# Hybrid encoder block: the residual's rows loaded in the gates' stage, a second spread of the norm, and float32 parts of the mixers ahead of float32r ones

## The chip, the cores and the metric

The kernel runs on one core of one Trainium2 chip. A core has a tensor engine (PE; its weight loads are shown apart as PEld), a vector engine (DVE), a scalar engine (ACT), GpSimd (POOL) and a sync engine (SP) that here issues loads. The metric is the device time of one execution in microseconds, lower is better. A profile shows one execution; its span runs from the first to the last record.

## The reference

256 tokens of 2048 channels go through one layer: norm, one input projection, two token mixers (windowed attention with 8 query and 2 key heads; dilated attention with 12 heads in 3 groups of strides 1, 4 and 16), a gate on each, output projection, gated MLP with a convolution of width 3 on the gate, and a gated per-layer embedding.

```python
h = rms_norm(x, attn_norm[i])
proj = h @ w_in[i]
qa, ka, va, qb, kb, vb, ga, gb = jnp.split(proj, split_points, axis=-1)
ya = windowed_gqa(qa, ka, va, rel_bias_table, sink_a[i])
yb = dilated_attention(qb, kb, vb, rel_bias_table)
merged = jax.nn.sigmoid(ga) * (ya @ w_branch_a[i]) + jax.nn.sigmoid(gb) * (yb @ w_branch_b[i])
x = x + merged @ w_out[i]
hf = rms_norm(x, ffn_norm[i])
g = dwconv_centred(hf @ w_ffn_gate[i], conv_w[i], conv_b[i])
x = x + (jax.nn.gelu(g) * (hf @ w_ffn_up[i])) @ w_ffn_down[i]
gate_p = jax.nn.sigmoid(rms_norm(x, ple_norm[i]) @ w_ple_gate[i])
x = x + gate_p * (p[i] @ w_ple_proj[i])
```

All of it is float32. The logits of all heads get a bias from a table by relative position; the windowed heads have a sink in their softmax.

## The kernel before

**Weights.** All weights come as blocks of 128 x 128 in one long stream, in the order in which they are used. `load` brings 16 blocks (1 MB, `raw`, three buffers) on the sync engine's queue; in the opening in halves of 8. `split_to` (L181) makes of each sub of 8 blocks a float32r part `whi` on ACT (L190) and the rest `wlo` on DVE (L191), four buffers each. A projection of one block of channels (`product`, L207) takes per block a matmul with `whi` over 512 moving columns (high and low part of the activations) and one with `wlo` over 256 (L201, L202), 16 blocks each. Where the weights are the moving side (`wide_product`, L214), each step has two token halves with three matmuls (L224, L225, L226).

**Stages.** In the opening, seven projections run side by side over the input's channels as these land, and are summed in seven PSUM banks `first`; a small product for the bias table (L396) follows. `gather` (L249) then empties each `first` bank: ACT copies one half to `t` (L252), DVE adds the other (L256, L258). The value product of the windowed heads comes next and takes over the banks of the first two. Then come the mixers: one projection after the other, with attention put between their blocks. Next are the gates' stage (four rounds of both gates and both branch projections), the output projection, the MLP in two halves, and the embedding.

**What sets the order.** `at((job, step), f)` puts a piece of work in front of that step of that projection, and `run_due` runs it there. For each head or group, `attend` (L506) puts `scores` (L431) at step 9 of a projection, `turn` (L472; softmax weights transposed, L481, and split into `near` and `far`) at step 11 or 12 of the next, and `values` (L489) at step 4 of the one after. Near parts (`thrice`, L424) are three float32r matmuls each, L427 to L429; far parts, which only the groups with three heads have, are plain float32 (L446, L496). A scheduler then orders each engine's instructions; it may move an instruction far ahead of where it is written, unless it is marked with `keep`. Each DMA signals on one of eight signals in turn, so that an issue waits for the one eight places earlier on both queues together.

**Rows of the residual.** `fetch` (L667) loads a piece of 128 x 512 of the input's rows on ACT's queue into the buffer `x`, whose channel-wise content is then spent. It is written at step 6 of each gate's projection: eight pieces of 256 KB.

**The norm.** `rms` (L307) has two parts: `ask` computes the root, `tell` spreads it over all partitions with one float32 matmul (L304) and a copy on ACT (L315). The MLP's norm is spread once, at step 9 of its second projection.

Of the kernel before, what the change touches and what calls it, by code (L numbers as in the profile page):

```python
# [16 lines left out]
P = 128  # L17
T = 256
# [93 lines left out]
START = FIRST + 1  # L112
_JOBS = _plan()
WARM = 9


def _stream():
# [16 lines left out]
def _encoder(ctx: ExitStack, tc, xt, pt, cols, table, onehot, mask, ident_in, last_gain, wts, xrows, out):  # L134
# [172 lines left out]
    def rms(i, total, key, n):  # L307

        def ask():
            rc[key], dg = norm(total(), n)  # L310

            def tell():
                b = spread(dg)
                rt[key] = sc.tile([P, T], F32, name="rms")
                nc.scalar.activation(rt[key], b, AF.Copy)  # L315
            at(i[1], tell)
        at(i[0], ask)


# [2 lines left out]
    def at(i, f, *a):  # L322

        due.setdefault(i, []).append((f, a))
# [12 lines left out]
    hb = big.tile([P, QH * AW + BH * BW], F32, name="mov")  # L337
    hba = hb[:, :QH * AW].rearrange("p (h c) -> p h c", c=AW)
    hbb = hb[:, QH * AW:].rearrange("p (h c) -> p h c", c=BW)
    oh = ap_.tile([NBUCK, 2 * T], F32, name="oh", tag="near", bufs=1)  # L340
    tb = sc.tile([NBUCK, NH], F32, name="tb", bufs=1)
    mk = ap_.tile([NH, 2 * T], F32, name="mk", tag="s1", bufs=2)

# [67 lines left out]
    def view(a, offset, *dims):  # L411
        return bass.AP(tensor=a.tensor, offset=a.offset + offset, ap=[a.ap[0], *([step, n] for step, n in dims)])
# [18 lines left out]
    def scores(heads, y):  # L431

        n = len(heads)
        wide = T if n == 1 else 2 * T
        s = ap_.tile([P, 2, wide], F32, name="s", tag="s%d" % n, bufs=2 if n == 1 else 1)
        h, k = heads[0]
        sp = ps.tile([P, 2, T], F32, name="sp", bufs=2)
        for t in range(2):
            thrice(sp[:, t, :], [qs[h][:, c + t * P:c + (t + 1) * P] for c in (0, T)], [ks[k][:, :T], ks[k][:, T:]])
        a, step = (hba[:, h, :], P) if n == 1 else (hbb[:, h - QH, :], 1)  # L440
        nc.vector.tensor_tensor(s[:, :, :T], sp, view(a, 0, (step, 2), (1, T)), op=ALU.add)
        if n > 1:
            sp = ps.tile([P, 2, T], F32, name="sp", bufs=2)
            for g, (h, k) in enumerate(heads[1:]):
                for t in range(2):
                    nc.tensor.matmul(sp[:, t, g * P:(g + 1) * P], qs[h][:, t * P:(t + 1) * P],  # L446
                                     ks[k][:, (1 - t) * P:(2 - t) * P], start=True, stop=True)
            for g, (h, k) in enumerate(heads[1:]):
                nc.vector.tensor_tensor(s[:, :, T + g * P:T + (g + 1) * P], sp[:, :, g * P:(g + 1) * P],
                                        view(hbb[:, h - QH, :], 1, (0, 2), (2, P)), op=ALU.add)  # L450
        mx = ap_.tile([P, 2], F32, name="mx")
        nc.vector.tensor_reduce(mx, s, axis=AX.X, op=ALU.max)
        nm = ap_.tile([P, 2], F32, name="nm")
        if n == 1:
            sk = sinks[:, y:y + 1]
            nc.vector.tensor_scalar(nm, mx, sk, -1.0, op0=ALU.max, op1=ALU.mult)
        else:
            nc.vector.tensor_scalar(nm, mx, -1.0, None, op0=ALU.mult)
        den = ap_.tile([P, 2], F32, name="den")
        for t in range(2):  # L460
            nc.scalar.activation(s[:, t, :], s[:, t, :], AF.Exp, bias=nm[:, t:t + 1], accum_out=den[:, t:t + 1])
        if n == 1:
            es = ap_.tile([P, 2], F32, name="es")
            nc.scalar.activation(es, nm, AF.Exp, bias=sk)
            nc.vector.tensor_tensor(den, den, es, op=ALU.add)
        rd = ap_.tile([P, 2], F32, name="rd")
        nc.vector.reciprocal(rd, den)
        for t in range(2):
            nc.vector.tensor_scalar(s[:, t, :], s[:, t, :], rd[:, t:t + 1], None, op0=ALU.mult)
        return s  # L470

    def turn(s):  # L472

        n = s.shape[-1] // P
        near = ap_.tile([P, 2, 2, T], FR, name="near", bufs=1)
        far = ap_.tile([P, 2, T], F32, name="far", bufs=1) if n > 2 else None
        for c in range(0, n, 2):
            p = ps.tile([P, 2, T], F32, name="pt", bufs=2)
            for k in range(2):
                for t in range(2):  # L480
                    nc.tensor.transpose(p[:, k, t * P:(t + 1) * P], s[:, t, (c + k) * P:(c + k + 1) * P], ident)  # L481
            if c:
                nc.scalar.activation(far, p, AF.Copy)
            else:
                nc.scalar.activation(near[:, 0], p, AF.Copy)
                nc.vector.tensor_tensor(near[:, 1], p, near[:, 0].bitcast(F32), op=ALU.subtract)
        return near, far

    def values(w, heads, y):  # L489
        near, far = w  # L490
        o = ps.tile([P, T], F32, name="misc")
        for t in range(2):
            thrice(o, vs[heads[0][1]][t], [near[:, c, t, :] for c in range(2)], t == 0, t == 1 and len(heads) == 1)
        for g, (_, k) in enumerate(heads[1:]):
            for t in range(2):
                nc.tensor.matmul(o[:, t * P:(t + 1) * P], vs[k][1 - t], far[:, g, t * P:(t + 1) * P],  # L496
                                 start=False, stop=(g == len(heads) - 2), skip_group_check=True)
        hi, lo = yab[:, y, :T], yab[:, y, T:]
        if len(heads) == 1:
            ov = o[:, ::-1]  # L500
        else:
            ov, hi, lo = paired(o, True), pairs(hi), pairs(lo)
        nc.scalar.activation(hi, ov, AF.Copy)
        nc.vector.tensor_tensor(lo, ov, hi.bitcast(F32), op=ALU.subtract)

    def attend(i, heads, y):  # L506
        def first():
            s = scores(heads, y)

            def second():  # L510
                w = turn(s)
                at((i + 1, 11) if end else (i + 3, 4), values, w, heads, y)
            at((i + 1, 8) if end else (i + 2, 11 if len(heads) == 1 else 12), second)
        end = y == QH + HG - 1
        at((i + 1, 3 if end else 9), first)
# [4 lines left out]
    def after(job, i, acc, u=None):  # L520
        ff = held.get("ff")
        kind, n = job[0], job[1]
        if kind in ("q", "k", "v"):
# [35 lines left out]
                        else:  # L559
                            nc.vector.tensor_tensor(o, pairs(u), paired(r.bitcast(F32), True), op=ALU.subtract)  # L560
            else:
                r = ap_.tile([P, T], F32, name=kind, bufs=4 if kind == "q" else 7)
                nc.vector.tensor_tensor(paired(r, kind == "q"), pairs(u), pairs(rt[0]), op=ALU.mult)
            if kind == "k":
                ks[n] = r
# [99 lines left out]
    res = x.rearrange("p k t -> p (k t)").rearrange("p (t n) -> p t n", t=2)  # L665

    def fetch(t, c):  # L667
        nc.scalar.dma_start(res[:, t, c * W4:(c + 1) * W4], xrows[t][:, c * W4:(c + 1) * W4])

    movers = {  # L670
        "q": lambda k: hs[:, k, :], "g": lambda k: held["hf"][:, k, :],
# [7 lines left out]
    for i, job in enumerate(_JOBS):  # L679
# [25 lines left out]
            held["lg"] = spare[:, 2 * D:3 * D]  # L705
            nc.scalar.dma_start(held["lg"], last_gain)
        if kind == "g" and n == 0:
            rms([(i, 14), (i + 1, 9)], lambda: rowsums(held["ss1"]), 1, 2)
        if kind in ("ga", "gb"):
            at((i, 6), fetch, int(kind == "gb"), n)  # L710
        if kind == "bb":
# [10 lines left out]
            nc.vector.tensor_scalar(held["half"], root(rowsums(held["ss2"]), 2), 0.5, None, op0=ALU.mult)  # L722
        if i < FIRST:
            firsts[i] = gather(firsts[i], SCALE if kind == "q" else 1.0,
                               ap_.tile([P, T], F32, name="first", tag="k", bufs=7), keep)
            continue
        if i == FIRST:
            rms([(START, 6), (START, 12)], lambda: sums(tot, HALVES + TWINS), 0, 4)
# [91 lines left out]
```

## Time and profile before

| | |
|---|---|
| runs shown | 1495.14, 1496.67, 1497.42 us; median 1496.67 |
| profiled execution | 1494.23 us, span 1492.4 us |
| busy share of PE, PEld, DVE, ACT | 99%, 85%, 65%, 49% |
| HBM read | 279.49 MB, 189 GB/s over the span |
| granted PE clock | 0.997 on average |

The page has the busy time of each engine, the span in 40 slices, the DMA queues, the chain of work that ended last, the costliest groups of instructions, and the DMA issues. A row of the timeline has start, duration, engine, line, operation, output and inputs, and in brackets the idle time before it and what ended it. "ACTq" and "SPq" are the queues in which ACT and SP issue DMAs. A float32 product has two records per matmul. The records of matmuls overlap: in a dense stream the next starts before the last one's modelled end.

### The profile page before, as it was taken

To read this page: it belongs to the slowest core of one execution; us is meant where nothing else is said; L and a number is where in the kernel's file an instruction comes from. 1 tells how busy PE (TensorE), PEld (TensorE's weight loads), DVE (VectorE), ACT (ScalarE), POOL (GpSimd) and SP (SyncE) were. 2 spreads that over 40 slices of the span, in tenths; PEclk is the share of its full clock that TensorE was granted. 3 is DMA by queue.
4 is the path that set the end of the run, shared out by engine and by line. 5 is a ranking of instruction groups with operands and counts; after the bars stand their busy time and mean duration, and the time that the engine had idled before them with its cause. 6 is when DMAs were issued, how large, how long until landed. Compare 5 with 4: busy or idle time off the path is not lost.

```text
span 1492.4 us, 19451 instructions
## 1 busy us (share of the span) xinstructions
PE 1478.4 (99%) x7616; PEld 1261.6 (85%) x7616; DVE 976.3 (65%) x1406; ACT 728.3 (49%) x1031; POOL 3.7 (0%) x9
## 2 busy tenths in 40 slices
PE   9999999999999999999999999999999999999997
PEld 8888888888888888888888888888888888888886
DVE  6596665664554555578888885447787887555565
ACT  7465444444444444555554554334545554444553
POOL 0000000000000000000000000000000000000000
PEclk9999999999999999999999999999999999999999
DMA  8844444445554455454455455555544544544552
GB/s 305 297 170 150 165 173 178 168 166 190 193 198 180 186 197 198 178 222 180 190 198 190 179 196 197 196 192 178 196 181 186 193 179 194 188 181 196 190 188 102
DMA packets 46376, 282.89 MB, mean 190 GB/s; under 512 B 5124, under 2 KB 9988, under 8 KB 14028
## 3 DMA queue, kind: packets, MB, share of 16 engines
q1 hardware_dynamic: 44268, 277.31, 49.7%
q10 hardware_dynamic: 2016, 4.33, 0.8%
q8 instruction: 60, 0.98, 0.3%
q14 instruction: 32, 0.26, 0.0%
HBM read 279.49 MB, written 2.14 MB: 189 GB/s over the span
## 4 chain that ended last, share of the span: by engine, by line
PE 95%; DMA 2%; DVE 1%; ACT 1%; issue 0%; SPq 0%; POOL 0%; ACTq 0%; POOLq 0%; DVEq 0%
PE acc L201 28%; PE acc L224 17%; PE acc L225 17%; PE acc L226 16%; PE acc L202 14%; DMA raw<-in_wts 2%; PE pt L481 0%; PE pt L601 0%; DMA x<-in_xrows 0%; DVE wlo L191 0%; ACT whi L190 0%; PE misc L496 0%; PE sp L446 0%; PE pt L622 0%; PE misc L427 0%
## 5 line engine op out<-in xcount | busy, mean ns | idle before, releaser
L191 DVE TENSOR_TENSOR wlo<-raw,whi 128x1024 fp32r<-128x1024 f32 (+1 forms) x519 | 631.8, 1218 | 477.7 <-ACT whi L190 477.2
L190 ACT ACTIVATE whi<-raw 128x1024 fp32r<-128x1024 f32 (+1 forms) x519 | 547.6, 1056 | 683.2 <-PE acc L226 356.3
L201 PE MATMUL acc<-mov,whi 128*128 128x512 f32 x1840 | 647.9, 396 | 0.0
L202 PE MATMUL acc<-mov,wlo 128*128 128x256 f32 x1840 | 515.6, 280 | 0.0
L201 PEld LDWEIGHTS acc<-mov,whi 128*128 128x128 f32 x1840 | 345.0, 188 | 79.9
L202 PEld LDWEIGHTS acc<-mov,wlo 128*128 128x128 f32 x1840 | 347.7, 189 | 0.5
L224 PE MATMUL acc<-whi,mov 128*128 128x512 f32 (+1 forms) x640 | 248.6, 388 | 2.4 <-DVE first L256 2.4
L225 PE MATMUL acc<-wlo,mov 128*128 128x512 f32 (+1 forms) x640 | 246.8, 386 | 0.0
L226 PE MATMUL acc<-whi,mov 128*128 128x512 f32 (+1 forms) x640 | 246.8, 386 | 0.0
L224 PEld LDWEIGHTS acc<-whi,mov 128*128 128x128 f32 x640 | 121.4, 190 | 26.4 <-DVE first L256 3.3
L226 PEld LDWEIGHTS acc<-whi,mov 128*128 128x128 f32 x640 | 121.4, 190 | 24.0
L225 PEld LDWEIGHTS acc<-wlo,mov 128*128 128x128 f32 x640 | 121.5, 190 | 23.0
L224 PE MATMUL acc<-whi,act 128*128 128x512 f32 x352 | 137.5, 391 | 0.0
L226 PE MATMUL acc<-whi,act 128*128 128x512 f32 x352 | 137.0, 389 | 0.0
L225 PE MATMUL acc<-wlo,act 128*128 128x512 f32 x352 | 136.9, 389 | 0.0
L226 PEld LDWEIGHTS acc<-whi,act 128*128 128x128 f32 x352 | 66.1, 188 | 13.9
L224 PEld LDWEIGHTS acc<-whi,act 128*128 128x128 f32 x352 | 66.1, 188 | 13.6
L225 PEld LDWEIGHTS acc<-wlo,act 128*128 128x128 f32 x352 | 66.1, 188 | 13.3
L252 ACT ACTIVATE t<-acc 128x256 f32<-128x256 f32 x115 | 42.1, 366 | 0.0
L256 DVE TENSOR_TENSOR u<-acc,t 128x256 f32<-128x256 f32 x100 | 41.6, 416 | 0.0
L201 PE MATMUL first<-mov,whi 128*128 128x512 f32 x112 | 39.2, 401 | 0.8 <-ACT whi L190 0.6
L226 PE MATMUL acc<-whi,yab 128*128 128x512 f32 x96 | 37.3, 389 | 0.0
(144 smaller groups left out, 908.9 us busy)
## 6 DMA issues: line engine op xcount, KB each, us to landing
raw<-in_wts SPq DMA_DIRECT2D x251, 1024.0 KB, 4.8
raw<-in_wts SPq DMA_DIRECT2D x12, 512.0 KB, 6.6
x<-in_xrows ACTq DMA_DIRECT2D x8, 256.0 KB, 5.9
x<-in_xt SPq DMA_DIRECT2D x13, 128.0 KB, 6.0
mov<-hold SPq DMA_DIRECT2D x3, 514.0 KB, 6.4
mov<-hold SPq DMA_DIRECT2D x2, 768.0 KB, 7.8
mov<-in_last_gain ACTq DMA_DIRECT2D x1, 1024.0 KB, 5.1
out<-x ACTq DMA_DIRECT2D x2, 384.0 KB, 3.5
```

The source lines that it names most:

```text
L190: nc.scalar.activation(hi, src, AF.Copy)
L191: nc.vector.tensor_tensor(lo, src, hi.bitcast(F32), op=ALU.subtract)
L201: nc.tensor.matmul(acc, hi[:, o, :], m, start=first, stop=False, skip_group_check=True)
L202: nc.tensor.matmul(acc[:, T:], lo[:, o, :], m[:, :T], start=False, stop=last, skip_group_check=True)
L224: nc.tensor.matmul(acc, xh, hi, start=(k == 0), stop=False)
L225: nc.tensor.matmul(acc, xh, lo, start=False, stop=False)
L226: nc.tensor.matmul(acc, xl, hi, start=False, stop=(k == n - 1))
L252: keep(nc.scalar.activation(t, acc[:, T:], AF.Copy, scale=scale))
L256: nc.vector.tensor_tensor(u, acc[:, :T], t, op=ALU.add)
```

## The change

`fetch` is marked with `keep`. The MLP's norm is spread a second time, at step 9 of the first projection of the second half (`_HALF`), into a new tile. In `scores` the far part stands ahead of the near one, in `values` it stands between the two halves of the near one. `values` of the first seven windowed heads moves from its own place to right behind the next head's transposes (`held["turned"]`). `near` (and `oh`, which shares its buffer) gets two buffers, far keys 5 instead of 7, far queries 2 instead of 4, and the seven results of the opening are spread over both.

```diff
+_HALF = next(i for i, j in enumerate(_JOBS) if j[0] == "g" and j[1] == FHALF)
...
-            at(i[1], tell)
+            for e in i[1:]:
+                at(e, tell)
         at(i[0], ask)
...
-    oh = ap_.tile([NBUCK, 2 * T], F32, name="oh", tag="near", bufs=1)
+    oh = ap_.tile([NBUCK, 2 * T], F32, name="oh", tag="near", bufs=2)
...
-        h, k = heads[0]
-        sp = ps.tile([P, 2, T], F32, name="sp", bufs=2)
-        for t in range(2):
-            thrice(sp[:, t, :], [qs[h][:, c + t * P:c + (t + 1) * P] for c in (0, T)], [ks[k][:, :T], ks[k][:, T:]])
-        a, step = (hba[:, h, :], P) if n == 1 else (hbb[:, h - QH, :], 1)
-        nc.vector.tensor_tensor(s[:, :, :T], sp, view(a, 0, (step, 2), (1, T)), op=ALU.add)
         if n > 1:
             sp = ps.tile([P, 2, T], F32, name="sp", bufs=2)
...
+        h, k = heads[0]
+        sp = ps.tile([P, 2, T], F32, name="sp", bufs=2)
+        for t in range(2):
+            thrice(sp[:, t, :], [qs[h][:, c + t * P:c + (t + 1) * P] for c in (0, T)], [ks[k][:, :T], ks[k][:, T:]])
+        a, step = (hba[:, h, :], P) if n == 1 else (hbb[:, h - QH, :], 1)
+        nc.vector.tensor_tensor(s[:, :, :T], sp, view(a, 0, (step, 2), (1, T)), op=ALU.add)
...
-        near = ap_.tile([P, 2, 2, T], FR, name="near", bufs=1)
+        near = ap_.tile([P, 2, 2, T], FR, name="near", bufs=2)
...
-            thrice(o, vs[heads[0][1]][t], [near[:, c, t, :] for c in range(2)], t == 0, t == 1 and len(heads) == 1)
-        for g, (_, k) in enumerate(heads[1:]):
-            for t in range(2):
-                nc.tensor.matmul(o[:, t * P:(t + 1) * P], vs[k][1 - t], far[:, g, t * P:(t + 1) * P],
-                                 start=False, stop=(g == len(heads) - 2), skip_group_check=True)
+            thrice(o, vs[heads[0][1]][t], [near[:, c, t, :] for c in range(2)], t == 0, t == 1)
+            for g, (_, k) in enumerate(heads[1:] if t == 0 else []):
+                for e in range(2):
+                    nc.tensor.matmul(o[:, e * P:(e + 1) * P], vs[k][1 - e], far[:, g, e * P:(e + 1) * P],
+                                     start=False, stop=False, skip_group_check=True)
...
                 w = turn(s)
-                at((i + 1, 11) if end else (i + 3, 4), values, w, heads, y)
+                if "turned" in held:
+                    values(*held.pop("turned"))
+                if y < QH - 1:
+                    held["turned"] = (w, heads, y)
+                else:
+                    at((i + 1, 11) if end else (i + 3, 4), values, w, heads, y)
...
-                r = ap_.tile([P, T], F32, name=kind, bufs=4 if kind == "q" else 7)
+                r = ap_.tile([P, T], F32, name=kind, bufs=2 if kind == "q" else 5)
...
-        nc.scalar.dma_start(res[:, t, c * W4:(c + 1) * W4], xrows[t][:, c * W4:(c + 1) * W4])
+        keep(nc.scalar.dma_start(res[:, t, c * W4:(c + 1) * W4], xrows[t][:, c * W4:(c + 1) * W4]))
...
-            rms([(i, 14), (i + 1, 9)], lambda: rowsums(held["ss1"]), 1, 2)
+            rms([(i, 14), (i + 1, 9), (_HALF, 9)], lambda: rowsums(held["ss1"]), 1, 2)
...
-                               ap_.tile([P, T], F32, name="first", tag="k", bufs=7), keep)
+                               ap_.tile([P, T], F32, name="first", tag="k" if i < 5 else "q", bufs=5 if i < 5 else 2),
+                               keep)
```

How the scheduler's order moves is shown at three places. Line numbers are each kernel's own; the changed kernel's are higher by one or two at L190 to L400.

ACT at the end of the opening, before the change (`sq_489` is the last square of the input, `whi` the splits, `t` the gathers of the seven banks):

```order
L367 ACTIVATE sq_489<-x 128x1024
L668 DMA x<-in_xrows 128x512
L190 ACTIVATE whi<-raw 128x1024
L668 DMA x<-in_xrows 128x512
L190 ACTIVATE whi<-raw 128x1024 x3
L252 ACTIVATE t<-first 128x256 x2
L190 ACTIVATE whi<-raw 128x1024
L252 ACTIVATE t<-first 128x256 x4
L190 ACTIVATE whi<-raw 128x1024
```

The same place in the changed kernel:

```order
L369 ACTIVATE sq_489<-x 128x1024
L191 ACTIVATE whi<-raw 128x1024 x3
L253 ACTIVATE t<-first 128x256 x2
L191 ACTIVATE whi<-raw 128x1024
L253 ACTIVATE t<-first 128x256 x2
L191 ACTIVATE whi<-raw 128x1024
L253 ACTIVATE t<-first 128x256 x3
```

The last two of the eight row loads stood here and are gone (all eight stood in the opening). The first of the three splits in the changed rows belongs to the opening, so two splits of the next weights stand ahead of the first gathers, where there were three.

DVE at the same place, before (`wlo` the rests of the splits, `first<-first,t` the gathers, `rows` the bias):

```order
L390 TENSOR_TENSOR tot<-squares 128x256
L191 TENSOR_TENSOR wlo<-raw,whi 128x1024 x3
L256 TENSOR_TENSOR first<-first,t 128x256 x2
L398 TENSOR_TENSOR rows<-misc,mk 20x512
L258 SCALAR_TENSOR_TENSOR first<-first,t 128x256 x2
```

And in the changed kernel:

```order
L392 TENSOR_TENSOR tot<-squares 128x256
L192 TENSOR_TENSOR wlo<-raw,whi 128x1024 x2
L257 TENSOR_TENSOR first<-first,t 128x256 x2
L192 TENSOR_TENSOR wlo<-raw,whi 128x1024
L259 SCALAR_TENSOR_TENSOR first<-first,t 128x256
L400 TENSOR_TENSOR rows<-misc,mk 20x512
```

The third `wlo` moved behind the two gathers that free the banks of the value product.

DVE in the middle of the windowed heads, before (`rd` and `s<-s,rd` end a head's softmax, `yab` is the result of an older head, `near` the split of the turned weights, `mx` and `nm` start the next head's softmax):

```order
L467 RECIPROCAL rd<-den 128x2
L504 TENSOR_TENSOR yab<-misc,yab 128x256
L469 TENSOR_SCALAR s<-s,rd 128x256 x2
L191 TENSOR_TENSOR wlo<-raw,whi 128x1024
L264 TENSOR_TENSOR kf<-u,kf 128x256
L264 TENSOR_TENSOR qf<-first,qf 128x256
L441 TENSOR_TENSOR s<-sp,mov 128x512
L486 TENSOR_TENSOR near<-pt,near 128x512
L452 TENSOR_REDUCE mx<-s 128x2
L456 TENSOR_SCALAR nm<-mx,cl 128x2
```

And in the changed kernel:

```order
L469 RECIPROCAL rd<-den 128x2
L257 TENSOR_TENSOR u<-acc,t 128x256
L471 TENSOR_SCALAR s<-s,rd 128x256 x2
L556 TENSOR_TENSOR u<-u,rms 128x256
L192 TENSOR_TENSOR wlo<-raw,whi 128x1024
L265 TENSOR_TENSOR kf<-u,kf 128x256
L265 TENSOR_TENSOR qf<-first,qf 128x256
L452 TENSOR_TENSOR s<-sp,mov 128x512
L488 TENSOR_TENSOR near<-pt,near 128x512
L454 TENSOR_REDUCE mx<-s 128x2
L506 TENSOR_TENSOR yab<-misc,yab 128x256
L458 TENSOR_SCALAR nm<-mx,cl 128x2
```

The write of `yab` moved from ahead of the scaling `s<-s,rd` to between the next head's maximum and its negative.

## Prediction

> **What bounds the kernel now.** I read the page first: busy shares, then the chain of work that ended last, then the waits of TensorE.
>
> ```profile
> span 1492.4 us, 19451 instructions
> ...
> PE 1478.4 (99%) x7616; PEld 1261.6 (85%) x7616; DVE 976.3 (65%) x1406; ACT 728.3 (49%) x1031; POOL 3.7 (0%) x9
> ...
> PE 95%; DMA 2%; DVE 1%; ACT 1%; issue 0%; SPq 0%; POOL 0%; ACTq 0%; POOLq 0%; DVEq 0%
> ```
>
> TensorE is busy for 99% of the span and is 95% of the chain. No part of the change takes a matmul away, so it can gain only where TensorE stands still or runs slowly. The view of waits lists all that it waited for:
>
> ```profile
> PE acc L224 <- DVE first L256: 2.4, 1, 2.4
> PE misc L157 <- DVE mhalf L152: 1.1, 1, 1.1
> PE first L201 <- ACT whi L190: 0.6, 1, 0.6
> PE first L201 <- DVE mov L269: 0.2, 1, 0.2
> ```
>
> The largest wait comes once, where the opening (seven projections, summed in the seven `first` banks) ends and the first value product begins. The timeline of TensorE there (start, duration, instruction, idle time before it and what ended it):
>
> ```profile
> 46.15 1.03 PE L396 MATMUL misc<-oh,tb 32*20 32x512 f32 x2
> 49.61 0.39 PE L224 MATMUL acc<-whi,mov 128*128 128x256 f32 x1 [2.43 <-DVE first L256]
> ...
> 51.05 0.41 PE L226 MATMUL acc<-whi,mov 128*128 128x256 f32 x1
> 51.26 0.41 PE L224 MATMUL acc<-whi,mov 128*128 128x256 f32 x1
> ...
> 53.73 0.28 PE L224 MATMUL acc<-whi,mov 128*128 128x256 f32 x1
> ```
>
> The windows by stretch (length, busy time and count for PE, PEld, DVE, ACT, POOL; then granted clock, DMA share, GB/s) and a piece of the chain add the clock and the end of that product:
>
> ```profile
> 50.00:51.00 1.00, 1.00 (x7) 1.00 (x7) 1.00 (x3) 0.47 (x2) 0.00 (x0) 0.59 0.89 360
> 51.00:52.00 1.00, 1.00 (x7) 1.00 (x6) 1.00 (x2) 0.55 (x2) 0.00 (x0) 0.50 0.79 328
> ```
> ```profile
> 62.88 0.23 PE acc L201
> ```
>
> So the hole has a second price. After 2.43 us of standing still TensorE gets half its clock until about 53.6 us: matmuls stand 0.21 us apart (51.05, 51.26). Why the hole is there, in the timelines of ScalarE, VectorE and the load queue, and in the load queue's waits:
>
> ```profile
> 36.39 0.36 ACTq L668 DMA_DIRECT2D x<-in_xrows  x1
> 44.41 2.01 ACT L190 ACTIVATE whi<-raw 128x1024 fp32r<-128x1024 f32 x2 [6.98 <-DMA raw<-in_wts]
> 46.91 1.06 ACT L190 ACTIVATE whi<-raw 128x1024 fp32r<-128x1024 f32 x1 [0.49 <-DMA raw<-in_wts]
> 47.87 0.64 ACT L252 ACTIVATE t<-first 128x256 f32<-128x256 f32 x2
> ```
> ```profile
> 45.50 3.72 DVE L191 TENSOR_TENSOR wlo<-raw,whi 128x1024 fp32r<-128x1024 f32 x3 [5.97 <-ACT whi L190]
> 49.14 0.75 DVE L256 TENSOR_TENSOR first<-first,t 128x256 f32<-128x256 f32 x2
> ```
> ```profile
> 36.70 11.52 SPq L174 DMA_DIRECT2D raw<-in_wts  x4
> ```
> ```profile
> SPq L355 <- DMA x<-in_xrows: 3.8, 1, 3.8
> SPq L358 <- DMA x<-in_xrows: 2.1, 1, 2.1
> SPq L360 <- DMA x<-in_xrows: 1.8, 1, 1.8
> ```
>
> The product needs two banks that `gather` frees (L252, then L256). L252 stands in ScalarE's queue behind three splits `whi` whose weights come late: ScalarE waits 6.98 us for one load and 0.49 us for the next. Those loads were issued from 36.70 us on, after the queue had stood 3.8 + 2.1 + 1.8 = 7.7 us behind loads of the residual's rows, two of which left just before them (the last at 36.39).
>
> **The change, part by part.** *Loads of the rows held back.* The eight loads leave the opening for the gates' stage. The next weights landed at 44.41. Two 256 KB loads less in front of them at 360 GB/s (the window's rate) are 1.5 us, and with the 7.7 us in the queue it is 9.2 at most: they land between 35.2 and 42.9 us. The four `whi` buffers let the two halves be split only when TensorE is done with the sub four places back, 24 and 16 blocks of 0.35 us (0.23 + 0.12) before 46.15: 37.7 and 40.5 us. The new order matters as much: ScalarE's gathers now stand behind two splits, not three, and VectorE's behind two `wlo`, not three. The first bank is full six blocks before 46.15, at 44.0; `gather` frees it 0.8 us later (0.32 and 0.38, halves of the 0.64 and 0.75 above, and the hand-over), and the second by about 45.4. At the late end (42.9) the two splits and two `wlo` of 1.2 us end at about 46.2 and the gathers at 47.0. Both come no later than the bias product's end. That product's record ends at 47.18, but a dense stream starts its next matmul 0.16 us before a record's modelled end (0.39 long and 0.23 apart, L201's step in the chain), at 47.02: 49.61 - 47.02 = **2.6 us gained**. What is late next at this place is TensorE itself.
>
> *The slow clock goes with the hole.* From 49.61 to 53.73 there are 21 matmuls, 4.12 us; the other 75 of the product's 96 (16 steps, two halves, three passes) take 62.88 - 53.73 = 9.15 us, 0.122 each. 21 x 0.122 = 2.56, so **1.6 us gained**.
>
> *The first load of rows* also stood in front of a split, in the timelines of ScalarE, the load queue and TensorE:
>
> ```profile
> 10.52 0.34 ACTq L668 DMA_DIRECT2D x<-in_xrows  x1
> 10.96 1.06 ACT L190 ACTIVATE whi<-raw 128x1024 fp32r<-128x1024 f32 x1 [0.47 <-DMA raw<-in_wts]
> ```
> ```profile
> 10.66 0.33 SPq L174 DMA_DIRECT2D raw<-in_wts  x1
> ```
> ```profile
> 12.07 1.65 PE L201 MATMUL first<-mov,whi 128*128 128x512 f32 x6 [0.62 <-ACT whi L190]
> ```
>
> The load queue's issue at 10.66 waits for the same landing as the split at 10.96. So the split can start 0.3 us earlier, and TensorE's 0.62 us becomes 0.32: **0.3 us gained** (bounds 0 and 0.47), kept because the opening is dense behind it.
>
> *The rows in the gates' stage.* Eight issues go into ScalarE's queue, with no wait in front of them, and 2.1 MB beside the weights. A window there:
>
> ```profile
> 340.00:350.00 10.00, 10.00 (x46) 8.29 (x45) 4.90 (x4) 3.38 (x4) 0.00 (x0) 1.00 0.57 210
> ```
>
> The DMA engines are at 0.57, ScalarE at 3.38 of 10, and TensorE waits for no load after the opening. I cost it at 0; without that cover it would be 2.1 MB at 360 GB/s, 5.8 us. The rows are read first in the output projection, at least 38 steps of six matmuls of 0.23 us behind the last load, 52 us.
>
> *The second spread* is one float32 matmul and a copy on ScalarE. The first one:
>
> ```profile
> 656.98 0.59 PE L304 MATMUL misc<-rdg,ones 128*128 128x256 f32 x2
> 657.23 0.58 PE L201 MATMUL acc<-mov,whi 128*128 128x512 f32 x1
> 657.64 0.28 PE L202 MATMUL acc<-mov,wlo 128*128 128x256 f32 x1
> ```
>
> From 656.98 to 657.64 is 0.66 us where one step of 0.23 would stand: **0.43 us lost**. The copy lies in ScalarE's idle half.
>
> *float32 parts ahead, and values behind the next head's transposes.* The same matmuls in another order. What a change from float32 to float32r costs shows behind the far scores:
>
> ```profile
> 165.12 1.05 PE L446 MATMUL sp<-k,q 128*128 128x128 f32 x8
> 165.93 0.48 PE L224 MATMUL acc<-whi,mov 128*128 128x512 f32 x1
> 166.25 0.40 PE L225 MATMUL acc<-wlo,mov 128*128 128x512 f32 x1
> ```
>
> The step behind it is 0.32 instead of 0.23, 0.09 us. Before and after, each of the 15 moved places (4 scores, 4 values of three groups, 7 values moved to a turn) has as many such changes as it had, so I take 0; if each gained or lost one it would be 1.4 us either way. Smaller pools (`k` 5, `q` 2) add no wait that I find: each group of heads needs two far keys and two far queries, and these are read one projection after they are made, several projections before their buffers are written again.
>
> Sum: -2.6 - 1.6 - 0.3 + 0.4 = **-4.1 us**. The profiled execution took 1494.23 us, 1.8 more than its span; it would take 1490.1 and the span 1488.3. The median of the runs shown is 1496.67, 2.4 above that execution; from it the forecast is **1492.6 us**, 0.27% faster.
>
> **The rivals.** *The slow clock isn't in the usual run.* The row for it: 2.43 us idle, then about 3.4 us at half clock. One execution can't show how often such a hole drops the clock. If the runs behind the median don't have it, only -2.6 - 0.3 + 0.4 = -2.5 us are left, 1494.2. The Trainium skill, page "TensorE: Matmul & The Clock Gate", section "Part 1: The HAM clock gate", says that the clock halves after at least one idle window of about 3.4 us, and that this window runs free of the kernel. The trace agrees on the length of the slow stretch, but its hole is shorter than that window; by that rule it would drop the clock in some runs only. Chance 0.27.
>
> *The hole closes in part.* The gathers still come late, since the next weights land late or a split holds ScalarE; half of 4.2 us stays, -2.0 us, 1494.7. Against it stand the 3 us of margin above. Chance 0.10. *Nothing to see*: the moved loads or the reordering give back what the opening gains (up to 5.8 and 1.4 us), 1496 to 1498. Against it: no wait of TensorE outside the opening. Chance 0.08.
>
> *Slower: the turn waits for its softmax.* Between 70 and 104 us VectorE is nearly full. The change puts the write of `yab` behind the maximum and ahead of `nm`, so each head's exponentials start behind the values just computed. The slack, on VectorE and TensorE:
>
> ```profile
> 94.10 0.61 DVE L469 TENSOR_SCALAR s<-s,rd 128x256 f32<-128x256 f32 x2
> ```
> ```profile
> 95.85 0.60 PE L481 MATMUL pt<-ident,s 128*128 128x128 f32 x4
> ```
>
> The scaled scores are ready at 94.71, 1.1 us ahead of the transposes. Beyond 1.1 us of slip each microsecond is paid by seven heads; slower by 3 us needs (3.0 + 4.1) / 7 = 1.0 us more, a slip of 2.1: 1499.7. Against it: the same write left its place ahead of L469, so the net is about 0, and six value matmuls of 0.12 us and one copy on ScalarE end before VectorE gets there. Chance 0.04.
>
> **How the numbers follow.** The forecast has 0.51, and everything better than it by more than its error is in that. A measurement of this kernel can tell about 0.2%, 3.0 us, from no change. Faster by more takes nearly all of the forecast's case and a quarter of the first rival's (the three runs lie 2.3 us apart, so a median is good for about 1): 0.57. Slower 0.04, the rest 0.39. The range goes from the forecast with 1.4 us gained by the reordering and 1.6 of noise, 1489.6, to the partial case with 1.1 of noise, 1495.8; the two last rivals and the ends are left out.
>
> **What would show it.** In the changed profile: the first value product behind the bias product with no wait, at about 46.7 us; granted clock 1.00 from 47 to 60; no wait of the load queue for the rows before 300 us; a second spread, at the start of the gated projections' second half, that costs 0.43; no new wait of TensorE from 70 to 330 us; span about 1488.3. A hole that stays, with `gather` late, would make the first part wrong, a slow clock without a hole the second; a wait of the transposes for VectorE would speak for the last rival.

## The result, and the profile after

| | before | after |
|---|---|---|
| median of the runs | 1496.72 us (4 runs, 1495.14 to 1497.42) | 1485.22 us (4 runs, 1485.03 to 1485.88) |
| profiled execution | 1494.23 us, span 1492.4 us | 1485.03 us, span 1483.1 us |

The ratio of the times is 0.9925, with a 95% interval from 0.9908 to 0.9943: 11.5 us less. The forecast was 1492.6 us, in a range that ended at 1489.6. The page of the changed kernel (the span, the busy line, the shares of the chain):

```profile
span 1483.1 us, 19449 instructions
...
PE 1472.1 (99%) x7618; PEld 1258.2 (85%) x7618; DVE 975.9 (66%) x1406; ACT 729.4 (49%) x1032; POOL 3.7 (0%) x9
...
PE 97%; DVE 1%; ACT 0%; DMA 0%; issue 0%; POOL 0%; ACTq 0%; POOLq 0%; DVEq 0%
```

TensorE's busy time fell by 6.3 us (1478.4 to 1472.1), although it has one matmul more (two records): part of the gain is not a wait that went, but work that runs closer together. The whole list of TensorE's waits is now

```profile
PE misc L158 <- DVE mhalf L153: 1.1, 1, 1.1
```

The hole behind the opening is gone. In the timeline of TensorE the first value product (now L225 to L227) follows the bias product (now L398), and the next narrow product (L202) follows 12.58 us after it:

```profile
45.27 1.03 PE L398 MATMUL misc<-oh,tb 32*20 32x512 f32 x2
46.24 0.39 PE L225 MATMUL acc<-whi,mov 128*128 128x256 f32 x1
...
57.85 0.40 PE L202 MATMUL acc<-mov,whi 128*128 128x512 f32 x1
```

Before, the same stretch went from 46.15 to 62.71, 16.56 us:

```profile
62.71 0.40 PE L201 MATMUL acc<-mov,whi 128*128 128x512 f32 x1
```

ScalarE's timeline shows why. The gathers (now L253) that stood behind three late splits start when TensorE has filled the banks, and no longer when weights land:

```profile
43.30 0.73 ACT L253 ACTIVATE t<-first 128x256 f32<-128x256 f32 x2 [2.52 <-PE first L203]
```

And the clock stays up. The windows of four microseconds behind it (length, busy time and count for PE, PEld, DVE, ACT, POOL; granted clock, DMA share, GB/s), before and after:

```profile
50.00:54.00 4.00, 4.00 (x23) 4.00 (x23) 2.94 (x6) 1.02 (x3) 0.00 (x0) 0.57 0.60 211
```
```profile
50.00:54.00 4.00, 4.00 (x35) 4.00 (x35) 1.84 (x2) 1.53 (x2) 0.00 (x0) 1.00 0.95 332
```

So far the change did what the prediction said. To find the rest, I took the start of each matmul of the same place in both traces, and the difference between them along the program. After the value product the changed kernel is 4.86 us ahead (0.88 of it already at the end of the opening, 3.98 in the stretch above), at the end of the mixers (330 us) 5.03, and still 5.03 at 1000 us. Then comes a second gain: 0.43 us are lost at the second spread, and between 1011 and 1260 us 4.68 are won, which brings it to 9.27 us. After that nothing changes. The windows of TensorE (length, busy time and count, granted clock, DMA share, GB/s) in the two halves of the MLP show it, first before the change:

```profile
700.00:800.00 100.00, 100.00 (x579) 1.00 0.51 190
1100.00:1200.00 100.00, 100.00 (x567) 1.00 0.50 189
```

and after it:

```profile
700.00:800.00 100.00, 100.00 (x579) 1.00 0.53 190
1100.00:1200.00 100.00, 100.00 (x579) 1.00 0.53 190
```

TensorE is busy for all of each window, at full clock and with nearly the same DMA load, and yet in the second half of before it does 2% fewer of the same matmuls. There are **two paces**: a pair of one 512-column matmul and one 256-column matmul takes 346.7 ns or 353.3 ns. Before, the first half ran at the short one and the second at the long one; after, both run at the short one. In the changed kernel's timeline the pace switches at the second spread (L305):

```profile
1009.61 0.40 PE L202 MATMUL acc<-mov,whi 128*128 128x512 f32 x1
...
1009.96 0.40 PE L202 MATMUL acc<-mov,whi 128*128 128x512 f32 x1
...
1010.31 0.40 PE L202 MATMUL acc<-mov,whi 128*128 128x512 f32 x1
...
1010.67 0.59 PE L305 MATMUL misc<-rdg,ones 128*128 128x256 f32 x2
1010.92 0.58 PE L202 MATMUL acc<-mov,whi 128*128 128x512 f32 x1
1011.33 0.28 PE L203 MATMUL acc<-mov,wlo 128*128 128x256 f32 x1
1011.45 0.40 PE L202 MATMUL acc<-mov,whi 128*128 128x512 f32 x1
...
1011.80 0.39 PE L202 MATMUL acc<-mov,whi 128*128 128x512 f32 x1
...
1012.14 0.40 PE L202 MATMUL acc<-mov,whi 128*128 128x512 f32 x1
```

Ahead of the spread the pairs start 0.35 and 0.36 us apart (in the trace's nanoseconds 350, 361, 349, over and over, 353.3 on average), behind it 0.35 and 0.34 (350 and 343 in turn, 346.7). The second half of the MLP has some 694 pairs behind that point; 694 x 6.67 ns = 4.6 us.

### The profile page after: what moved, and what is told of

Same layout as the page of the kernel before. It is cut to its first block, busy times and chain, and to the rows that moved or that the text cites. A ratio compares the mean times of both kernels' runs of the same rounds, so it can differ in the third digit from the quotient of the medians.

```text
span 1483.1 us, 19449 instructions
## 1 busy us (share of the span) xinstructions
PE 1472.1 (99%) x7618; PEld 1258.2 (85%) x7618; DVE 975.9 (66%) x1406; ACT 729.4 (49%) x1032; POOL 3.7 (0%) x9
## 4 chain that ended last, share of the span: by engine, by line
PE 97%; DVE 1%; ACT 0%; DMA 0%; issue 0%; POOL 0%; ACTq 0%; POOLq 0%; DVEq 0%
PE acc L202 28%; PE acc L225 17%; PE acc L226 17%; PE acc L227 17%; PE acc L203 14%; PE first L202 2%; PE first L203 1%; PE pt L483 0%; PE pt L608 0%; DVE wlo L192 0%; PE sp L442 0%; PE misc L498 0%; PE pt L629 0%; DMA x<-in_xt 0%; PE misc L429 0%; PE misc L430 0%
## 5 line engine op out<-in xcount | busy, mean ns | idle before, releaser
L202 PE MATMUL acc<-mov,whi 128*128 128x512 f32 x1840 | 642.1, 394 | 0.0
L202 PEld LDWEIGHTS acc<-mov,whi 128*128 128x128 f32 x1840 | 344.7, 187 | 77.5
L225 PE MATMUL acc<-whi,mov 128*128 128x512 f32 (+1 forms) x640 | 247.6, 387 | 0.0
L227 PE MATMUL acc<-whi,mov 128*128 128x512 f32 (+1 forms) x640 | 246.2, 385 | 0.0
L225 PEld LDWEIGHTS acc<-whi,mov 128*128 128x128 f32 x640 | 120.8, 189 | 24.0 <-DVE wlo L192 0.8
L227 PEld LDWEIGHTS acc<-whi,mov 128*128 128x128 f32 x640 | 120.7, 189 | 24.0
L225 PE MATMUL acc<-whi,act 128*128 128x512 f32 x352 | 137.5, 391 | 0.0
L227 PE MATMUL acc<-whi,act 128*128 128x512 f32 x352 | 137.0, 389 | 0.0
L227 PEld LDWEIGHTS acc<-whi,act 128*128 128x128 f32 x352 | 66.1, 188 | 13.9
L225 PEld LDWEIGHTS acc<-whi,act 128*128 128x128 f32 x352 | 66.1, 188 | 13.6
L253 ACT ACTIVATE t<-acc 128x256 f32<-128x256 f32 x115 | 42.1, 366 | 0.0
L202 PE MATMUL first<-mov,whi 128*128 128x512 f32 x112 | 38.6, 397 | 0.2
L225 PE MATMUL acc<-whi,yab 128*128 128x512 f32 x96 | 37.3, 389 | 0.0
```

Of the source, the lines that this page charges most:

```text
L202: nc.tensor.matmul(acc, hi[:, o, :], m, start=first, stop=False, skip_group_check=True)
L225: nc.tensor.matmul(acc, xh, hi, start=(k == 0), stop=False)
L227: nc.tensor.matmul(acc, xl, hi, start=False, stop=(k == n - 1))
L253: keep(nc.scalar.activation(t, acc[:, T:], AF.Copy, scale=scale))
```

## The experiments

### Is it the spread, and what of it?

Four kernels. The second spread added to the kernel before, with nothing else:

```diff
-            at(i[1], tell)
+            for e in i[1:]:
+                at(e, tell)
...
-            rms([(i, 14), (i + 1, 9)], lambda: rowsums(held["ss1"]), 1, 2)
+            rms([(i, 14), (i + 1, 9), (_HALF, 9)], lambda: rowsums(held["ss1"]), 1, 2)
```

> The kernel before with the second spread of the norm alone (one float32 matmul of 256 columns and its copy, at step 9 of the first projection of the MLP's second half). Theory A, the float32 matmul switches the narrow product stream behind it from 353.3 to 346.7 ns per pair: the stretch from 1012 to 1271 us gets 4.2 us shorter, the opening keeps its hole of 2.43 us, median 4 us below the kernel before (about 1492.5). Theory C, the gain of that stretch comes from the other edits (rows, mixers): +0.4 us, no gain. The hole's slow clock stays in either case.

The second spread taken out of the changed kernel:

```diff
-            rms([(i, 14), (i + 1, 9), (_HALF, 9)], lambda: rowsums(held["ss1"]), 1, 2)
+            rms([(i, 14), (i + 1, 9)], lambda: rowsums(held["ss1"]), 1, 2)
```

> The changed kernel without the second spread. Theory A: the second half of the MLP runs at 353.3 ns per pair throughout, 4.2 us more than the changed kernel, about 1489.5 by the median and 7 us below the kernel before. Theory C: as the changed kernel less 0.4 us, about 1484.8.

The kernel before with its matmul alone:

```diff
             at(i[1], tell)
+            if key:
+                at((_HALF, 9), spread, dg)
```

> The kernel before with the spread's float32 matmul alone at that place: its result is read by nobody, no copy, no new tile. Theory A: -4.2 us, all of it between 1012 and 1271 us, 346.7 ns per pair there. Rival B, the new copy of the norm's spread (its other place in the buffer) makes VectorE or ScalarE cheaper and so the stream: +0.4 us, 353.3 ns.

And with its copy alone:

```diff
+            def again():
+                new = sc.tile([P, T], F32, name="rms")
+                nc.scalar.activation(new, rt[key], AF.Copy)
+                rt[key] = new
+            if key:
+                at((_HALF, 9), again)
```

> The kernel before with a copy of the norm's spread into a new tile on ScalarE at that place, and no matmul; the second half's projections read the new tile. Theory A: 0 us, 353.3 ns per pair from 1012 to 1260 us. Rival B: about -4.6 us, 346.7 ns.

| | median, us | kernel before in the same comparison | ratio, 95% interval | matmuls from 1100 to 1200 us |
|---|---|---|---|---|
| spread alone | 1492.89 | 1496.78 | 0.9968 [0.9956, 0.9980] | 579 |
| changed kernel without it | 1490.28 | 1496.78 | 0.9956 [0.9944, 0.9968] | 568 |
| matmul alone | 1491.85 | 1496.78 | 0.9966 [0.9953, 0.9979] | 579 |
| copy alone | 1496.55 | 1496.78 | 0.9995 [0.9986, 1.0004] | 568 |

The rows behind the last column, from the windows of the kernels with the matmul alone and with the copy alone:

```profile
1100.00:1200.00 100.00, 100.00 (x579) 1.00 0.53 190
```
```profile
1100.00:1200.00 100.00, 100.00 (x568) 1.00 0.52 184
```

The matmul does it, the copy and its new tile do nothing. Against the trace of before, the stretch from 1020 to 1271 us is 4.60 us shorter with the spread alone and with the matmul alone, and 0.00 with the copy alone. The rival that lays it to VectorE, ScalarE or the buffer falls, and so does the one that lays it to the other edits.

These runs also showed what the profile of before could not. Each kernel that keeps the rows in the opening has the hole, but not of one size, and the slow clock doesn't last equally long either. With the spread alone, in the list of waits and in the windows:

```profile
PE acc L224 <- DVE first L256: 4.7, 1, 4.7
```
```profile
50.00:54.00 4.00, 0.48 (x2) 0.48 (x3) 3.87 (x6) 3.38 (x7) 0.00 (x0) 0.67 0.62 211
54.00:56.00 2.00, 2.00 (x11) 2.00 (x11) 2.00 (x4) 0.93 (x3) 0.00 (x0) 0.50 0.99 414
56.00:58.00 2.00, 2.00 (x12) 2.00 (x11) 0.85 (x3) 0.00 (x0) 0.00 (x0) 0.50 0.38 78
```

Before, the clock was at half for 3.4 us, from 50.2 to 53.6. Here it is for 6.8 us, from 51.4, still inside the hole, to 58.2.

### The rows alone, and the mixers alone

> The kernel before with the row loads held in the gates' stage alone. The four kernels that keep the rows in the opening all show a hole (2.4 to 4.7 us) and half the clock behind it; theory: the held rows take both away, no wait of TensorE for L256, clock 1.00 from 46 to 60 us, and the narrow stream from 1012 to 1260 us stays at 353.3 ns per pair. From the opening alone 5 to 7 us, median about 1490.5. Rival: the order of the mixers or the two buffers of `near` are what moves the first value product; then the hole stays and the time is within 1 us of the kernel before.

```diff
-        nc.scalar.dma_start(res[:, t, c * W4:(c + 1) * W4], xrows[t][:, c * W4:(c + 1) * W4])
+        keep(nc.scalar.dma_start(res[:, t, c * W4:(c + 1) * W4], xrows[t][:, c * W4:(c + 1) * W4]))
```

> The changed kernel with the rows back in the opening and without the second spread: the reordered mixers and the pools alone. Theory: within 1 us of the kernel before; the hole of 2.4 to 4.7 us is there, half clock behind it; the mixers from 70 to 330 us gain 0.2 us. Rival: the two buffers of `near` or the order free the first banks early; no hole, 5 us.

The second kernel is the changed one with that line and the spread's line taken back. The rows alone gave 1490.68 us against 1496.49 (ratio 0.9962, 0.9949 to 0.9976); the mixers and pools alone 1495.32 against 1496.49 (0.9995, 0.9985 to 1.0004). TensorE's timeline with the rows alone:

```profile
46.68 1.03 PE L396 MATMUL misc<-oh,tb 32*20 32x512 f32 x2
47.64 0.39 PE L224 MATMUL acc<-whi,mov 128*128 128x256 f32 x1
...
59.26 0.40 PE L201 MATMUL acc<-mov,whi 128*128 128x512 f32 x1
```

And the wait of the mixers alone:

```profile
PE acc L225 <- DVE first L257: 5.1, 1, 5.1
```

The held rows close the hole by themselves; the two buffers of `near` and the order of the mixers don't. From the start of the bias product to the next narrow product, the seven kernels profiled with held rows take 12.57 or 12.58 us. The seven with the rows in the opening (before, spread alone, matmul alone, copy alone, mixers alone, and the first and third kernel of pieces below) take 16.56, 19.35, 18.41, 18.17, 19.67, 17.72 and 17.12 us: 4.0 to 7.1 more, 5.6 on average. The bias product itself starts at 46.25 us on average with held rows (45.27 to 47.73) and at 47.05 without (46.15 to 47.83). The mixers from 63 to 330 us are 0.62 us shorter with the mixers alone, and 0.17 in the changed kernel.

### What switches the pace

First, ten pieces of matmul in the second half of the kernel before, and ten in that of the changed one; nobody reads what they compute:

```diff
+            def probe(kind, count, cols):
+                hf = held["hf"][:, 0, :]
+                for _ in range(count):
+                    o = ps.tile([P, 2 * T], F32, name="misc")[:, :cols]
+                    if kind == "r":
+                        keep(nc.tensor.matmul(o, hf[:, :P], hf[:, :cols], start=True, stop=True))
+                    elif kind == "t":
+                        keep(nc.tensor.transpose(o, dg[:, :P], ident))
+                    else:
+                        keep(nc.tensor.matmul(o, ones, dg[:, :cols], start=True, stop=True))
+            if key:
+                for e, p in PROBES:
+                    at((_HALF + e, 9), probe, *p)
```

> The kernel before with ten small pieces of matmul put at step 9 of projections 3, 7, 11, ... of the MLP's second half, results read by nobody: one float32r matmul of 256 columns, one of 512, one float32 of 128 columns, one float32 of 256, the same again, two of 256 behind each other, one float32 transpose of 128 columns, four, two float32r of 256, three float32r of 256. Read is the pace of the pairs behind each. Theory A1 (a float32 matmul sets the fast pace): the float32r ones change nothing, the stream goes from 353.3 to 346.7 ns per pair behind the first float32 one and stays there. Theory A2 (a float32 matmul toggles): fast and slow in turn behind each. Theory C (any odd number of matmuls toggles): the pace changes behind the very first float32r one.

> The changed kernel with ten pieces in the same manner, from the fast pace: float32 of 256 columns, again, float32r of 256, float32r of 512, float32 of 128, four float32 transposes of 128, float32 of 256, float32r of 128, float32 of 128, one transpose. Theory A1: 346.7 ns per pair throughout. Theory A2: slow behind the first, fast behind the second, and so on at each float32 one. Theory C: a change behind each odd number of matmuls, of either type.

All three theories fell. In the first kernel a float32r matmul of 256 columns was enough to reach 346.7 ns, and the next one, of 512 columns, led back to 353.3. In the second, a float32 matmul of 256 columns left the short pace as it was twice, while one of 128 columns ended it. (Where several pieces were meant to stand together, a pair or half a pair came between them; those places are left out below.) So neither the type alone nor an odd count decides. A third kernel had 21 single matmuls:

> The kernel before with 21 single matmuls at step 9 of projections 1, 3, 5, ... 41 of the MLP's second half, in this order: float32r of 256 columns (r256), r128, r256, r512, r256, f128 (float32), r256, r128, r128, r512, r512, f256, f128, f256, r512, f256, r128, f256, r256, r256, one float32 transpose (t). Neither type alone (A1, A2) nor an odd count (C) fitted the twenty pieces tried so far. Theory D, the stream has steady patterns (346.7 or 353.3 ns per pair) and each kind of inserted matmul leaves it in one of them whatever came before: r256 and f256 always fast (6 r256 and 4 f256 here), r128 and f128 always slow (4 and 2), the transpose leaves what was. Theory E, where it lands depends on the pattern it came from: some r256 or f256 would leave the slow pace or some r128 the fast one, and r512 goes either way.

Theory D fell too: two float32 matmuls of 256 columns left the stream at 353.3 ns, and three float32r of 128 columns took it to 346.7. What fits is theory E, with the place in the pattern. At the long pace the pairs go 350, 361, 349 ns, in a cycle of three; at the short pace they go 346.7 each, or 350 and 343 in turn. All single pieces of the three kernels, with the second spread (f is float32, r float32r, t a transpose, then the columns; in brackets how often it was seen):

| the stream before it | goes to 346.7 ns | goes to, or stays at, 353.3 ns |
|---|---|---|
| long pace, behind the 361 ns pair | f256 (3), r256 (1), r128 (3) | r512 (1), t128 (1) |
| long pace, behind the 350 ns pair | r512 (1) | f256 (2), r256 (1) |
| long pace, behind the 349 ns pair | | r256 (1), f128 (2) |
| short pace, 346.7 each | f256 (2), r256 (2), r512 (3), t128 (2) | f128 (1) |
| short pace, 350 and 343 | f256 (3), r256 (3) | f128 (2), r128 (2), r512 (1) |

No piece at the same place in a pattern did one thing once and another thing another time. As one example, the timeline of the third kernel at a float32r matmul of 128 columns (L323): the pairs start 0.36 us apart in front of it, and 0.35 and 0.34 behind the first one.

```profile
1033.23 0.40 PE L201 MATMUL acc<-mov,whi 128*128 128x512 f32 x1
...
1033.59 0.22 PE L323 MATMUL misc<-mov 128*128 128x128 f32 x1
1033.65 0.45 PE L201 MATMUL acc<-mov,whi 128*128 128x512 f32 x1
...
1034.06 0.40 PE L201 MATMUL acc<-mov,whi 128*128 128x512 f32 x1
...
1034.41 0.39 PE L201 MATMUL acc<-mov,whi 128*128 128x512 f32 x1
...
1034.75 0.40 PE L201 MATMUL acc<-mov,whi 128*128 128x512 f32 x1
```

### The place of the spread

If that is so, the second spread gains by where it happens to stand. At step 9 it stands behind the 361 ns pair (1010.31 to 1010.67 above). Two kernels move it:

```diff
-            rms([(i, 14), (i + 1, 9), (_HALF, 9)], lambda: rowsums(held["ss1"]), 1, 2)
+            rms([(i, 14), (i + 1, 9), (_HALF, 8)], lambda: rowsums(held["ss1"]), 1, 2)
```

> The changed kernel with the second spread one step earlier, at step 8 of the same projection. Theory E (the stream's slow pattern is a cycle of three pairs, 350, 361 and 349 ns, and where an inserted matmul falls in it decides): at step 9 the spread stands behind the 361 ns pair, at step 8 behind the 350 ns one, and behind that one two f256 of the last run left the stream slow. So 353.3 ns per pair from 1012 to 1260 us, 4.6 us more than the changed kernel from there, median about 1490. Theory A1 (the spread as such sets the fast pace): as the changed kernel, 1485.2.

> The changed kernel with the second spread three steps later, at step 12: one whole cycle of three pairs on, so again behind the 361 ns pair. Theory E: fast from there, as the changed kernel, 1485.2 (0.02 us more for three slow pairs). A theory in which any shift from step 9 is bad, or chance decides: 353.3 ns, about 1490.

| second spread at | median, us | ratio, 95% interval | matmuls from 1100 to 1200 us |
|---|---|---|---|
| step 8 | 1490.57 | 0.9961 [0.9947, 0.9975] | 569 |
| step 12 | 1485.84 | 0.9930 [0.9918, 0.9943] | 579 |

The kernel before took 1497.06 us beside them. One step earlier, the gain is gone; three steps later, it is there. The timeline with the spread at step 8:

```profile
1010.53 0.40 PE L202 MATMUL acc<-mov,whi 128*128 128x512 f32 x1
...
1010.88 0.40 PE L202 MATMUL acc<-mov,whi 128*128 128x512 f32 x1
...
1011.23 0.59 PE L305 MATMUL misc<-rdg,ones 128*128 128x256 f32 x2
1011.47 0.58 PE L202 MATMUL acc<-mov,whi 128*128 128x512 f32 x1
...
1012.01 0.40 PE L202 MATMUL acc<-mov,whi 128*128 128x512 f32 x1
...
1012.37 0.40 PE L202 MATMUL acc<-mov,whi 128*128 128x512 f32 x1
```

The spread is the same instruction with the same cost (the next pair is 0.54 us long here, 1011.47 to 1012.01, and 0.53 above), but it stands behind a pair of 0.35 us, and the 0.36 us pair (1012.01 to 1012.37) comes back behind it. From 1020 to 1271 us this kernel loses 4.47 us to the changed one.

### A version that uses it

```diff
-            rms([(i, 14), (i + 1, 9), (_HALF, 9)], lambda: rowsums(held["ss1"]), 1, 2)
+            rms([(i, 14), (i + 1, 9)], lambda: rowsums(held["ss1"]), 1, 2)
...
+    def nudge(tag, m):
+        o = ps.tile([P, 2, T], F32, name=tag, bufs=2)[:, 0, :P] if tag == "pt" else ps.tile([P, T], F32, name=tag)[:, :P]
+        keep(nc.tensor.matmul(o, m[:, 0, :P], m[:, 0, :P], start=True, stop=True))
+
+    for e in ((20, 7), (34, 7)):
+        at(e, nudge, "pt", hs)
...
+        if i == _HALF:
+            at((i, 3), nudge, "misc", held["hf"])
```

> The changed kernel without the second spread; in its place one float32r matmul of 128 columns, its result read by nobody, at step 3 of the second half's first projection, and two more of them in the mixers, at the places where long stretches run at 353.3 ns per pair (step 7 of projections 20 and 34, each behind a 361 ns pair). Theory E (r128 behind the 361 ns pair led to the fast pace three times of three): -0.3 us for the cheaper switch in the second half, -0.45 and -0.3 in the mixers, each as 6.7 ns on 77 and 56 pairs less 0.06, so about 1.0 us below the changed kernel in the trace, 1484.2. Theory A1 (only the float32 matmul of 256 columns sets it): the second half slow, 1489.6.

It took 1484.91 us (1484.37 to 1485.47), ratio 0.9923 (0.9909 to 0.9937); its neighbour with the spread at step 12 took 1485.58 to 1486.67 on the same chip, so it is some 0.9 us ahead of that one. Along the program it gains 0.39, 0.26 and 0.35 us on the changed kernel at the three places, 1.00 in all, and loses 0.31 of it in the start of the opening, which differs from run to run. The first place, in the windows of this version and of the changed kernel:

```profile
181.00:210.00 29.00, 29.00 (x169) 1.00 0.48 179
```
```profile
181.00:210.00 29.00, 29.00 (x165) 1.00 0.49 179
```

## Why the prediction was wrong

*The hole and the slow clock: right in mechanism, under-sized.* The prediction had 2.6 + 1.6 = 4.2 us. Between the two profiled executions the stretch lost 16.56 - 12.58 = 3.98, nearly that, by the steps described. The two splits ahead of the gathers ran early (from 36.94 and 39.72 us), ScalarE then stood idle for 2.52 us, the gathers began when the banks were full, and TensorE had no wait and clock 1.00. The terms measure 2.5 and 1.5: the value product starts 0.07 us before the end of the bias product's record, not 0.16, and it takes 11.62 us instead of 13.10. (The chain's row at 62.88, taken as its end, is 0.17 us late; the next product starts at 62.71.)

But the terms came from one execution and were then taken from the median of others. That execution lost least of the seven: 3.98 us, where the seven average 5.6. TensorE's idle time, 2.43 us in it, is 3.7 on average, and the value product behind it loses 1.8 instead of 1.5. That fits its lying 2.4 us under its median, a gap that the prediction noted and carried along as if it had nothing to do with the terms.

The rival that the clock's dip is rare falls: it came with all seven holes, from 2.43 us on. The mean granted clock of all runs agrees: of the 42 runs of the kernel before that stand beside the experiments, 25 had 0.995 or 0.996, 16 had 0.997 and one 0.998; of the 29 runs with held rows, 25 had 0.998, three 0.997 and one 0.999. The Trainium skill ("TensorE: Matmul & The Clock Gate", "Part 1: The HAM clock gate") asks for at least one idle window of about 3.4 us. Three of the holes seen here are shorter (2.4, 3.1 and 3.2 us), and the clock fell with each. In five of the seven it fell 2.4 to 3.0 us after the end of the bias product's record, so counted from there the limit doesn't hold here. Whether the bias product in front (1.03 us, on 32 of the rows and 20 of the columns) counts as work is not tested; counted from its start, the clock fell after 3.5 us or more in all seven.

*The first load of rows: 0.3. Right in direction, its size not settled.* The wait that this term stands for, of TensorE for a split at 12 to 14 us, is 0.62 to 1.04 us in all seven kernels with the rows in the opening; with held rows it is gone in five and 0.45 and 0.48 us in two. The opening ends 0.8 us earlier on average with held rows, but single kernels of each kind lie 1.7 to 2.5 us apart. Part of that is the pace: the opening's last 85 pairs took 29.57 us in three of the held kernels and 30.12 in the other four. Between the two profiled executions 0.55 of the opening's 0.88 us are of that kind.

*The rows in the gates' stage: 0, right.* From 330 to 640 us, over the gates' stage and the output projection, the difference between the traces stays at 5.03 us.

*The second spread: "0.43 us lost". This step failed.* The cost beside it was right: 1010.67 to 1011.33 is 0.66 us where a 0.23 step would stand. But the step took the stream around the matmul as fixed. It isn't: this matmul, behind a 361 ns pair, took the 694 pairs behind it from 353.3 to 346.7 ns, 4.6 us, and the sum of the term is -4.2 instead of +0.4. The trace of before held a clue that the prediction didn't use: the two halves of the MLP had 579 and 567 matmuls in 100 us with the same clock and nearly the same DMA share. The first spread was read for its cost only, and no row of the list of waits shows such a loss.

*The order in the mixers: 0, with bounds of 1.4 either way. Right.* Measured are 0.2 to 0.6 us gained. What the trace shows at work is the pace, not the price named, a change of type: the new order leaves the stream at the short pace behind the values of windowed heads, and at the long one behind the groups' scores (211 to 219 and 272 to 279 us in the changed kernel, at the short one before). The largest piece is the stretch from 250 to 270 us, at 346.7 ns where 353.2 stood before, 0.3 us.

*The forecast as a whole.* By parts: 5.6 for the hole and its clock, about 0.8 for the opening, 0.2 for the mixers, 4.2 for the pace make 10.8 of the 11.5 us; the rest is inside the interval (8.5 to 13.8 us). With the terms of the hole at their average alone the forecast would have been about 1491. The pace is what put the time below the range: the changed kernel without the second spread, 1490.28 us, lies inside it. That the stretch from 1012 us on gained at all was luck of the place, step 9 and not step 8.

What stays open: why the pairs have a cycle of three at all, and what in TensorE holds it. The trace shows that each weight load starts 2.5 to 3 ns behind a matmul on average at either pace, and that the 512-column step is 230 to 232 ns on average at the short pace and 236 at the long one, with 115 to 117 for the other. No run here tells more. Nor does any show what decides the opening's pace: the changed kernel ran it at the short one, and without the second spread, which comes 960 us later, at the long one.

## What to carry to other kernels

Where an engine is busy for 99%, count its instructions per 100 us in stages that do the same work: two stages with equal clock and DMA load and different counts hide a loss that no list of waits shows. An inserted instruction may change everything behind it, so measure a small insertion at several places, one step apart, before its gain is believed or its loss accepted. And before a hole is priced from one profile, look how that execution lies to the median of its runs; where it is 2 us under it, the hole may be larger in the others.

## What the hardware showed that was not expected

A dense stream of float32r matmuls of 512 and 256 columns has two steady paces, 346.7 and 353.3 ns per pair (1.9% apart), with granted clock 1.00 in both. It keeps one over hundreds of matmuls and across projections, and a single matmul of 128 to 512 columns switches it or not by its kind and by where in the pattern it stands: the same float32 matmul gained 4.6 us at step 9, gained as much at step 12, and gained nothing at step 8. TensorE's clock fell to half with an idle time of 2.43 us, and stayed there for 3.4 us behind four of the seven holes and 6.8 us behind the three others.
